# The squares of x's rows ahead of the activations' sums, and the first weight piece on another queue, in a fused encoder layer

## Chip, cores and metric

The kernel runs on one core of one Trainium2 chip. The metric is the device time of one execution in microseconds (us). A core has a matrix engine (TensorE, PE; its weight loads are listed as PEld), VectorE (DVE), ScalarE (ACT), GpSimd (POOL) and SyncE (SP), which only issues transfers here. Each engine runs its own list of instructions in order and waits on semaphores for the others. Transfers (DMAs) are issued by an engine's instruction and carried out by 16 shared DMA engines; the rows named SPq, ACTq and POOLq are the issuing side of those engines.

## What is computed

One layer of a bidirectional encoder on x of shape (512, 1024), float32:

```python
h = _rmsnorm(x, g_pre_mix)
proj = h @ w_in
q, k, v, g, u, sv, a_ret, a_sgu = jnp.split(proj, ...)
y_ret = _retention_branch(q, k, v, g, ret_decay_logit, w_ret_o)
y_sgu = _sgu_branch(u, sv, sgu_ln_g, sgu_ln_b, w_spatial, b_spatial, w_sgu_o)
merged = jax.nn.sigmoid(a_ret) * y_ret + jax.nn.sigmoid(a_sgu) * y_sgu
x = x + _rmsnorm(merged @ w_out, g_post_mix)
h2 = _rmsnorm(x, g_pre_ffn)
x = x + _rmsnorm(_conv_gated_mlp(h2, w_up, conv_w, conv_b, w_down), g_post_ffn)
```

What matters for this change is the first line. The norm divides each row of x by the root of its mean square. The kernel doesn't form h: it multiplies x, scaled by g_pre_mix, with the weights, and applies the factor of each row (`rstd`) to the products afterwards. So the squares of x's rows are needed only when the first products are to be scaled.

## The kernel before

**Numbers in two halves.** All large products are made of three matmuls (`mm3`). Each operand is split into a high half, rounded to the type fp32r by a copy on ScalarE (`copy`, L71), and a low half, the difference, made on VectorE (`tensor_sub` in `split`, L78). Weights come from one array `wall` of 146 blocks of 128 by 1024. `w_block` loads a block (L109), rounds it and forms its low half. Block 0 is loaded in three pieces, of 128, 384 and 512 columns (L122), so that TensorE can start on the first columns early; the first piece is rounded on VectorE (L123), the others on ScalarE. Raw blocks rotate through 4 buffers (one of them is kept by `hold` for the first microseconds), the halves through 9.

**Order of the work.** The text asks for weight blocks ahead of their use (`w_get`). A scheduler in the framework makes one list of instructions for each engine when the program is built: it goes by the place in the text, and takes an instruction from further down when it reckons that those before it aren't ready. Tiles come from pools by tag. The large tag is `blk` (74 tiles of 128 by 512), which serves the halves of x, the scaled copies, the sums, the rows of x, the q and k products and most of the rest; `tmp` has 6 tiles; constants have a tile each. PSUM has 8 banks in rotation (`ps`).

**The stages that the change touches.**
1. The parameters (`part`) are loaded on ScalarE's queue (L173). ScalarE then loads its function table and makes one small copy (`wact`). TensorE runs 18 warm-up matmuls (L213).
2. The q and k projection: for k from 0 to 7, `load_x` brings xT[k] (L189, a block of x transposed) and rounds it with its gain (L191); `x_low` forms the low half (L197); the matmuls of block k go into all 8 PSUM banks, `qk[0]` to `qk[7]` (L227 for block 0, `mm3` at L167 to L169 behind it). In between, `x_scaled` makes a scaled copy `xg[k]` of xT[k] on ScalarE (L204).
3. The activations' sums (`x_forms`, L245 to L260): for each of 4 pairs of scaled copies, four half-width additions on VectorE (L249 to L252), then two splits, whose roundings are on ScalarE and whose low halves are on VectorE. Their results are operands of the gate products (L612), much later.
4. Constants, then the squares by rows (L279 to L285): eight loads of half a row block of x (L282, on SyncE's queue, into `blk` tiles), and for each a Square on ScalarE that adds up along the row (L283). VectorE adds the two halves (L286), and `rsqrt` on POOL (L273, L276) makes `rstd`.
5. The logarithms of the decays (L291 to L312), small work on VectorE.
6. The eight PSUM banks are copied out (`qkraw`, `blk` tiles; L319 on VectorE for odd m, L71 on ScalarE for even m).
7. Four small matmuls (L327) spread rstd over a PSUM bank, which is the first bank that the copies of stage 6 set free. ScalarE copies it to `rbc`, which scales the rotary tables, loaded at L338 and L339.
8. `prep` (rotary) on VectorE, and beside it the first group of `t_group` on TensorE (L430 to L432), which takes four more of those banks.

All later stages (retention, spatial gating, gates, output projection, feed-forward) keep their text.

Of the kernel before, what the change touches and what calls it, by code (L numbers as in the profile page):

```python
# [15 lines left out]
P = 128  # L16
# [24 lines left out]
def tile_block(ctx: ExitStack, tc, xT, x, wall, par, cs, decay, wsp, bsp, gpost, gffn, out):  # L41
    nc = tc.nc
# [5 lines left out]
    def nm(s):  # L48
        uid[0] += 1
        return f"{s}_{uid[0]}"  # L50

    def blk(dt=F32, n="blk", shape=(P, S)):
        return sb.tile(list(shape), dt, tag="blk", bufs=NBLK, name=nm(n))
# [7 lines left out]
    def small(n, w, bufs=2):  # L61
        return sb.tile([P, w], F32, tag=n, bufs=bufs, name=nm(n))
# [4 lines left out]
    def const(n, shape):  # L67
        return sb.tile(list(shape), F32, tag=n, bufs=1, name=n)
# [4 lines left out]
    def as32(t):  # L73
        return t.bitcast(F32)

    def split(hi, lo, src):
        copy(hi, src)
        nc.vector.tensor_sub(lo, src, as32(hi))  # L78
# [6 lines left out]
    i = 0  # L85
# [13 lines left out]
    def raw_tile():  # L99
        return sb.tile([P, 1024], F32, tag="raw", bufs=4, name=nm("raw"))  # L100

    def slot(n, at=0):
        return sb.tile([P, 1088], F32R, tag="w4", bufs=9, name=nm(n))[:, at : at + 1024]

    def w_block(i):
        raw = raw_tile()
        resident = RES0 <= i < RES1 or i >= NW - RES_DOWN
        if i > 0:
            nc.sync.dma_start(raw, wall[i])  # L109
        if resident:  # L110
            hi, lo = [], []
            for c in range(2):
                h_, l_ = blk(F32R, "wh"), blk(F32R, "wl")
                split(h_, l_, raw[:, c * S : (c + 1) * S])
                hi.append(h_)
                lo.append(l_)
        else:
            hi, lo = slot("wh"), slot("wl")
            if i == 0:
                pieces = [slice(0, P), slice(P, S), slice(S, 2 * S)]  # L120
                for f in pieces:
                    nc.sync.dma_start(raw[:, f], wall[i, :, f])  # L122
                    (nc.vector.tensor_copy if f.start == 0 else copy)(hi[:, f], raw[:, f])  # L123
                for f in pieces:
                    nc.vector.tensor_sub(lo[:, f], raw[:, f], as32(hi[:, f]))
            else:
                split(hi, lo, raw)
        return hi, lo
# [24 lines left out]
    def w_get(look=LOOK):  # L153

        i = w_pos[0]
        w_pos[0] += 1
        room = 2 * look + (2 if units[i][0] == "blk" else 0)
        n = sum(w_size(u) for u in units[i : w_pos[1]])
        while w_pos[1] < len(units) and (w_pos[1] <= i or n + w_size(units[w_pos[1]]) <= max(room, 9 if look == LOOK else 0)):
            u = units[w_pos[1]]  # L160
            w_ready[w_pos[1]] = w_block(u[1]) if u[0] == "blk" else w_form(*u)
            w_pos[1] += 1
            n += w_size(u)
        return w_ready.pop(i)
# [6 lines left out]

    part = const("part", [P, NPAR])
    nc.scalar.dma_start(part, par)  # L173


    wact = const("wact", [P, 16])
# [68 lines left out]
    def x_forms(k):  # L245

        a, b = xg[k], xg[k + 4]
        s_ = blk(n="xs")
        nc.vector.tensor_sub(s_[:, T0], a[:, T1], b[:, T1])  # L249
        nc.vector.tensor_sub(s_[:, T1], s_[:, T0], a[:, T0])  # L250
        nc.vector.tensor_sub(a[:, T0], a[:, T0], a[:, T1])
        nc.vector.tensor_add(a[:, T1], b[:, T0], s_[:, T1])  # L252
        for names, s_ in (("S1", "S2"), s_), (("S3", "S4"), a):
            h_, l_ = blk(F32R, "sh"), blk(F32R, "sl")
            split(h_, l_, s_)
            for n, t in zip(names, (T0, T1)):
                forms[n].append((h_[:, t], l_[:, t]))

    for k in range(4):
        x_forms(k)  # L260

    ident = const("ident", [P, P])
    make_identity(nc, ident)
    ones = const("ones", [P, P])
# [5 lines left out]
    def rsqrt(o, v, scale, w):  # L270

        t = small("rs", 16, 4)
        nc.gpsimd.tensor_scalar(  # L273
            out=t[:, :w], in0=v, scalar1=scale, scalar2=EPS, op0=ALU.mult, op1=ALU.add
        )
        nc.gpsimd.tensor_tensor(out=o, in0=t[:, :w], in1=nhalf[:, :w], op=ALU.pow)  # L276
# [9 lines left out]
    nc.vector.tensor_add(ss[:, :NT], ss[:, :NT], ss[:, NT : 2 * NT])  # L286
    rstd = const("rstd", [P, NT])
    rsqrt(rstd, ss[:, :NT], 1.0 / D, NT)


    lgt = const("lgt", [P, 8])  # L291
# [23 lines left out]
    raw = []  # L315
# [582 lines left out]
    for t in range(NT):  # L898
        q = small("q", 2, 4)
        z = sb.tile([P, 1088], F32, tag="w4", bufs=9, name=nm("z"))[:, :D]  # L900
        for n in range(2):
            f = slice(n * S, (n + 1) * S)
# [107 lines left out]
```

## Time and profile before

| | us |
|---|---|
| median of 3 runs | 858.49 (856.82 to 858.81) |
| the profiled execution, its own time | 857.87 |
| its span, first to last instruction | 856.1 |
| PE / DVE / ACT / POOL busy | 838.8 / 547.2 / 377.5 / 70.1 |
| mean granted TensorE clock | 0.993 |

The profile is of one execution. Its rows give the start in us from the span's beginning, the length, the engine, the line of the kernel, the operation, and the tiles written and read, as output<-input. A bracket names how long the engine had been idle and what ended that idle time. An entry like x8 counts instructions put together in one row. The chain of waits goes back from the last instruction, at each step to what released it; what lies on that chain sets the time. The granted clock is 1.00 when TensorE's clock runs at full speed and 0.50 at half.

### The profile page before, as it was taken

Reading aid. Unit: us, or ns where it says so; the run is one execution under the profiler, and the core shown is the slowest. Engines: PE = TensorE matmul, PEld = TensorE weight load, DVE = VectorE, ACT = ScalarE, POOL = GpSimd, SP = SyncE. Lnnn points to the kernel's source line nnn. Section 1 sums busy time; section 2 is a strip of 40 time slices with the busy share of each in tenths; the row PEclk is TensorE's granted clock in tenths of the full one; section 3 lists DMA queues with packets and bytes.
Section 4 is the critical chain, followed back from the end, with each engine's and each line's share of the span. In section 5 each row is a group of like instructions: output and inputs, shape, how many; then the busy total and the mean of one; then the engine's idle time right before and its main releaser. Section 6 shows DMA issues by size and latency. Waiting matters only on the chain.

```text
span 856.1 us, 11249 instructions
## 1 busy us (share of the span) xinstructions
PE 838.8 (98%) x4444; PEld 722.1 (84%) x4444; DVE 547.2 (64%) x846; ACT 377.5 (44%) x605; POOL 70.1 (8%) x75
## 2 busy tenths in 40 slices
PE   8969999999999999999999999999999999999996
PEld 6858888888899999999988898888888888888885
DVE  5767987875698777767764766666666666322304
ACT  6554446444565544344444564444444444211301
POOL 0010000001222011123210100000000000000000
PEclk9989999999999999999999999999999999999999
DMA  8452222120234322222357033222222222222202
GB/s 269 154 200 83 74 75 75 54 95 25 62 99 149 99 99 81 93 99 99 127 162 278 1 96 102 99 98 99 99 99 98 99 97 91 97 90 96 96 1 99
DMA packets 27125, 87.88 MB, mean 103 GB/s; under 512 B 3072, under 2 KB 3712, under 8 KB 27072
## 3 DMA queue, kind: packets, MB, share of 16 engines
q1 hardware_dynamic: 25920, 84.82, 29.5%
q0 software_dynamic: 432, 1.32, 0.6%
q10 hardware_dynamic: 720, 1.02, 0.3%
q8 instruction: 35, 0.57, 0.3%
q14 instruction: 18, 0.15, 0.1%
HBM read 85.05 MB, written 2.10 MB: 102 GB/s over the span
## 4 chain that ended last, share of the span: by engine, by line
PE 94%; DVE 3%; ACT 1%; DMA 1%; issue 0%; POOL 0%; SPq 0%; POOLq 0%; DVEq 0%; ACTq 0%
PE ps L167 15%; PE ps L168 15%; PE ps L169 15%; PE ps L612 11%; PE ps L758 6%; PE ps L759 6%; PE ps L757 6%; PE ps L430 5%; PE ps L431 5%; PE ps L432 5%; DVE wf L78 2%; DMA raw<-wall 1%; PE ps L227 1%; PE ps L682 1%; PE ps L555 0%
## 5 line engine op out<-in xcount | busy, mean ns | idle before, releaser
L78 DVE TENSOR_TENSOR wl<-raw,wh 128x1024 fp32r<-128x1024 f32 (+1 forms) x131 | 149.1, 1149 | 160.4 <-PE ps L168 70.5
L71 ACT ACTIVATE wh<-raw 128x1024 fp32r<-128x1024 f32 (+2 forms) x133 | 129.1, 982 | 100.6 <-PE ps L759 45.3
L169 PE MATMUL ps<-h2h,wl 128*128 128x512 f32 (+1 forms) x384 | 142.3, 371 | 0.0
L168 PE MATMUL ps<-h2l,wh 128*128 128x512 f32 (+1 forms) x384 | 142.2, 371 | 0.0
L167 PE MATMUL ps<-h2h,wh 128*128 128x512 f32 (+1 forms) x384 | 142.2, 372 | 0.0
L71 ACT ACTIVATE wf<-raw 128x512 fp32r<-128x512 f32 x84 | 50.7, 627 | 80.5 <-issue 25.8
L78 DVE TENSOR_TENSOR wf<-raw,wf 128x512 fp32r<-128x512 f32 x84 | 67.3, 818 | 26.8 <-ACT wf L71 26.5
L168 PEld LDWEIGHTS ps<-h2l,wh 128*128 128x128 f32 x384 | 72.3, 188 | 12.6
L167 PEld LDWEIGHTS ps<-h2h,wh 128*128 128x128 f32 x384 | 72.1, 188 | 12.7 <-ACT h2h L823 0.3
L169 PEld LDWEIGHTS ps<-h2h,wl 128*128 128x128 f32 x384 | 72.2, 188 | 12.4
L430 PE MATMUL ps<-wh,xh 128*128 128x512 f32 x192 | 75.3, 392 | 0.0
L431 PE MATMUL ps<-wl,xh 128*128 128x512 f32 x192 | 75.1, 391 | 0.0
L432 PE MATMUL ps<-wh,xl 128*128 128x512 f32 x192 | 74.9, 390 | 0.0
L612 PE MATMUL ps<-sh,wf 128*128 128x256 f32 x384 | 72.8, 280 | 0.2 <-ACT u L71 0.2
L757 PE MATMUL ps<-wh,fh 128*128 128x512 f32 x176 | 68.5, 389 | 0.0
L758 PE MATMUL ps<-wl,fh 128*128 128x512 f32 x176 | 68.5, 389 | 0.0
L759 PE MATMUL ps<-wh,fl 128*128 128x512 f32 x176 | 68.5, 389 | 0.0
L866 ACT ACTIVATE cv<-ps,part 128x512 f32<-128x512 f32 x44 | 34.3, 780 | 76.3 <-PE ps L169 76.3
L612 PEld LDWEIGHTS ps<-sh,wf 128*128 128x128 f32 x384 | 60.8, 188 | 0.9 <-ACT u L71 0.6
L612 PE MATMUL ps<-xh,wf 128*128 128x256 f32 x288 | 54.6, 281 | 0.0
L612 PE MATMUL ps<-sl,wf 128*128 128x256 f32 x192 | 53.6, 279 | 0.0
L612 PEld LDWEIGHTS ps<-xh,wf 128*128 128x128 f32 x288 | 45.5, 188 | 0.4
(240 smaller groups left out, 1532.6 us busy)
## 6 DMA issues: line engine op xcount, KB each, us to landing
raw<-wall SPq DMA_DIRECT2D x145, 512.0 KB, 3.3
x<-x SPq DMA_DIRECT2D x16, 256.0 KB, 6.0
xT<-xT SPq DMA_DIRECT2D x8, 256.0 KB, 5.2
out<-z SPq DMA_DIRECT2D x4, 256.0 KB, 2.0
out<-z ACTq DMA_DIRECT2D x3, 256.0 KB, 2.5
cs<-cs SPq DMA_DIRECT2D x2, 256.0 KB, 3.8
gpm<-gpost POOLq DMA_DIRECT2D x2, 256.0 KB, 3.5
gpf<-gffn POOLq DMA_DIRECT2D x2, 256.0 KB, 3.6
```

Of the source, the lines that this page charges most:

```text
L71: nc.scalar.activation(out=o, in_=i, func=AF.Copy)
L78: nc.vector.tensor_sub(lo, src, as32(hi))
L167: nc.tensor.matmul(o, ah, bh, start=start, stop=False)
L168: nc.tensor.matmul(o, ah, bl, start=False, stop=False)
L169: nc.tensor.matmul(o, al, bh, start=False, stop=stop)
L430: nc.tensor.matmul(acc[t], xh[k][:, c], wh[:, f], start=k == 0, stop=False)
L431: nc.tensor.matmul(acc[t], xh[k][:, c], wl[:, f], start=False, stop=False)
L432: nc.tensor.matmul(acc[t], xl[k][:, c], wh[:, f], start=False, stop=k == KD - 1)
L612: nc.tensor.matmul(o, w_[:, c], a_, start=first and k == n == 0, stop=k == 3 and n == 2, skip_group_check=True,)
L757: nc.tensor.matmul(o, ah, bh, start=k == 0, stop=False)
L758: nc.tensor.matmul(o, ah, bl, start=False, stop=False)
L759: nc.tensor.matmul(o, al, bh, start=False, stop=k == self.nk - 1)
```

## The change

Two edits. The call of `x_forms` for the four pairs moves from ahead of the constants to behind `rsqrt(rstd, ...)`, so that in the text the eight loads and squares of x's rows, their sum and rstd now come ahead of the activations' sums. And the raw buffer of weight block 0 is taken at the very start of the text, where its first piece (128 columns, 64 KB) is issued on ScalarE's queue, behind `part`; the other two pieces stay on SyncE's queue, behind xT[0].

```diff
     def w_block(i):
-        raw = raw_tile()
+        raw = raw_tile() if i else raw0
...
                 for f in pieces:
-                    nc.sync.dma_start(raw[:, f], wall[i, :, f])
+                    if f.start:
+                        nc.sync.dma_start(raw[:, f], wall[i, :, f])
                     (nc.vector.tensor_copy if f.start == 0 else copy)(hi[:, f], raw[:, f])
...
     part = const("part", [P, NPAR])
     nc.scalar.dma_start(part, par)
+    raw0 = raw_tile()
+    nc.scalar.dma_start(raw0[:, 0:P], wall[0, :, 0:P])
...
-    for k in range(4):
-        x_forms(k)
-
     ident = const("ident", [P, P])
...
     rstd = const("rstd", [P, NT])
     rsqrt(rstd, ss[:, :NT], 1.0 / D, NT)
+    for k in range(4):
+        x_forms(k)
```

## The prediction

> **What bounds the kernel now.** I read the page's busy shares first, then the chain of waits around the places the diff touches, then each engine's timeline there, then a table by stretches.
>
> ```profile
> PE 838.8 (98%) x4444; PEld 722.1 (84%) x4444; DVE 547.2 (64%) x846; ACT 377.5 (44%) x605; POOL 70.1 (8%) x75
> ```
>
> TensorE (PE) works through 98% of a span of 856.1 us. So an edit pays only where TensorE stands still or runs at half clock. The chain of waits (start, length, what) shows two such places near the change. The first is the start:
>
> ```profile
> 0.73 0.38 SPq L189
> 1.17 0.42 SPq L122
> 1.64 5.30 DMA raw<-wall
> 6.96 0.53 ACT wh L71
> 7.54 7.17 PE ps L227 x23
> ```
>
> SyncE's queue (SPq) issues xT[0], then the pieces of weight block 0. The second piece (columns 128 to 511) sets the end: 5.30 us in flight, a rounding copy on ScalarE at 6.96, and TensorE starts at 7.54. From there to the end of the projection TensorE is full. In the rows of stretches the columns are length, PE busy, PEld, DVE, ACT, POOL, granted clock, DMA share and GB/s:
>
> ```profile
> 11.46:52.40 40.94, 40.94 (x182) 33.86 (x181) 31.32 (x70) 25.20 (x39) 0.00 (x0) 1.00 0.65 225
> 52.80:59.70 6.90, 0.01 (x1) 0.01 (x1) 3.64 (x6) 6.66 (x17) 1.30 (x3) 0.72 0.55 195
> 59.70:61.50 1.80, 1.80 (x9) 1.80 (x9) 1.24 (x2) 0.00 (x0) 1.76 (x3) 0.50 0.03 9
> ```
>
> The second place is the hole right behind: from 52.80 to 59.70 TensorE does nothing, and then it works at clock 0.50. The chain through that hole:
>
> ```profile
> 52.56 0.24 PE ps L169
> 52.82 1.06 ACT wh L71
> 53.88 3.06 ACT x L283 x10
> 56.94 0.48 ACT qkraw L71
> 57.42 0.62 ACT x L283 x2
> 58.60 1.06 POOL rstd L276
> 59.70 2.08 PE ps L327 x8
> 61.77 0.43 PE ps L430
> ...
> 62.93 0.23 PE ps L430
> ```
>
> ScalarE rounds a weight block (52.82), squares six halves of x's rows (L283, 0.61 us each), copies one sum out of PSUM between them, then POOL makes rstd, and only then may TensorE spread rstd (L327) and begin the next group (L430). (Each square counts twice, with the read of its accumulator: x10 is five.) The squares need x alone, and yet six of eight run after the projection.
>
> Why are the squares so late? SyncE's timeline and the page's list of landings:
>
> ```profile
> 32.12 0.33 SPq L109 DMA_DIRECT2D raw<-wall  x1
> 37.56 0.33 SPq L109 DMA_DIRECT2D raw<-wall  x1
> 43.26 0.33 SPq L109 DMA_DIRECT2D raw<-wall  x1
> 43.64 3.90 SPq L282 DMA_DIRECT2D x<-x  x8
> ```
> ```profile
> x<-x SPq DMA_DIRECT2D x16, 256.0 KB, 6.0
> ```
>
> The eight loads of x's rows are issued from 43.64 to 47.5, behind three weight loads that the text places elsewhere, and take 6.0 us to land. Two squares fit before the weight rounding of 52.82; six stand behind it. The loads need nothing from the chip, so something else held them. My reading: x's rows lie in tiles of the large shared pool (tag blk), and its tiles are handed out in the order of the text, so the loads waited for the sums' tiles. Two rows speak for it:
>
> ```profile
> L657 POOL DMA_DIRECT2D bst<-bsp x1: 626/626/626, 224.5 to 224.5; - x1
> ```
> ```profile
> 62.67 0.33 SPq L655 DMA_DIRECT2D wst<-wsp  x1
> ```
>
> Two neighbouring loads of the text: the one into a blk tile waits until 224.5, although POOL is 8% busy; the one into a tile of its own goes at 62.67.
>
> **The change, part by part.** *1. Squares ahead of the sums.* No instruction is added or removed; eight loads, eight squares, the addition (L286) and POOL's rstd move ahead of the sums (x_forms). By the reading above the loads may now go once the last scaled copy of xT has its tile:
>
> ```profile
> 32.64 1.94 ACT L204 ACTIVATE xg<-xT,part 128x512 f32<-128x512 f32 x3
> ```
> ```profile
> 33.44 0.42 DVE L249 TENSOR_TENSOR xs<-xg,xg 128x256 f32<-128x256 f32 x1
> 36.28 1.23 DVE L78 TENSOR_TENSOR wl<-raw,wh 128x1024 fp32r<-128x1024 f32 x1 [0.44 <-PE ps L168]
> ...
> 49.29 0.69 DVE L78 TENSOR_TENSOR sl<-xg,sh 128x512 fp32r<-128x512 f32 x1
> ...
> 52.65 1.22 DVE L78 TENSOR_TENSOR wl<-raw,wh 128x1024 fp32r<-128x1024 f32 x1 [2.68 <-issue]
> 53.80 1.28 DVE L319 COPY qkraw<-ps 128x512 f32<-128x512 f32 x2
> ```
>
> That tile is given at about 33.9 (the third of three copies from 32.64). On SyncE's queue the loads then stand between the weight loads of 32.12 and 37.56: eight issues at 3.90/8 = 0.49 us fill 33.0 to 37.5. They move past two weight loads (37.56 and 43.26), which delays the first by some tenths; its block is rounded only at 52.82, so that is covered. Landing 6.0 us later, the last square ends near 44, and rstd (0.16 + 0.19 + 1.06 us on DVE and POOL, by the distance from 58.04, where the last square's 0.62 ends, to 59.66) is there near 46. No wait on rstd is left at 52.80.
>
> What is late next? First, the sums. Before, they ran from 33.44 to 49.98 on VectorE, 16.5 us with three weight blocks' low halves among them:
>
> ```profile
> L78 DVE TENSOR_TENSOR wl<-raw,wh 128x1024 fp32r<-128x1024 f32 x3 | 3.7, 1220 | 0.4 <-PE ps L168 0.4
> ```
>
> Without these they take 12.9 us. Now they wait for the tiles of x's rows and start, I estimate, at 36 to 37.5, behind the low half of 36.28. With two low halves (2.4 us) and up to 1 us for ScalarE's eight squares (4.9 us) crossing their splits, they end at 52 to 54. That is the edge of the hole, and the copies of the sums out of PSUM (qkraw, blk tiles too) stand behind them now, where they stood behind the squares before. The old cover for the sums was 10 us of slack up to 59.7; the new one is nearly nothing.
>
> Second, TensorE's next instruction (L327) writes a PSUM bank that the first qkraw copy must empty. That copy is on ScalarE, and the rounding of the weight block, free at 52.82, may stand ahead of it: 1.06 + 0.48 gives 54.36, plus 0.05: TensorE idles from 52.80 to 54.4, 1.6 us. The bound below is 0 (copies made during the projection's last matmuls, since all banks but the last are complete before its end), the bound above is the old hole. I take 1.6, because the sums' estimated end falls on 52 to 54 and the rounding becomes free just there. The next banks follow on VectorE: the low half of 52.65 ends at 53.9, two copies of 0.64 by 55.2, beside L327.
>
> Third, the price of the whole hole. From 52.80 to 62.93 TensorE did L327 (2.08 us at half clock, 1.04 at full, by the clock row) and three matmuls, at full clock 0.23 each as the row at 62.93: together 1.73 us of work in 10.13 us. So 8.4 us are lost there, and 8.4 - 1.6 = **6.8 us** come back, if the clock stays full.
>
> ```profile
> 4.63:8.03 3.40, 1.15 (x6) 0.63 (x4) 1.46 (x3) 0.62 (x2) 0.00 (x0) 1.00 0.86 225
> 8.05:11.44 3.39, 3.39 (x9) 2.38 (x9) 1.53 (x3) 2.36 (x4) 0.00 (x0) 0.50 0.91 350
> ...
> 52.42:55.82 3.40, 0.36 (x2) 0.00 (x0) 2.42 (x3) 3.00 (x8) 0.00 (x0) 1.00 0.59 210
> 55.84:62.64 6.80, 2.94 (x11) 2.75 (x12) 3.69 (x8) 4.44 (x12) 3.06 (x5) 0.50 0.33 118
> ```
>
> These stretches are cut on the grid on which the granted clock changes in this trace; they are multiples of 3.4 us. A stretch with 0.36 us of TensorE work and one with 1.15 of 3.40 were each followed by half clock; full stretches by full clock. With an idle 1.6 us the stretch from 52.42 holds about 1.8 us of work, 0.65 above the nearest row that lost the clock and 1.6 below a full one. I take full clock; losing it costs half of 3.4, 1.7 us. The Trainium skill, "TensorE: Matmul & The Clock Gate", section "What's actually happening", says that the clock falls to half after an idle window of about 3.4 us, in windows that run freely; by that an idle of 1.6 us would lose nothing. The trace is stricter: 2.25 us of idle in a window sufficed at 4.63.
>
> Behind the hole nothing new binds: TensorE's stretch from 62.66 starts with its operands there, and the sums are first read by the products of L612, behind all groups of t_group.
>
> *2. First piece on ScalarE's queue.*
>
> ```profile
> 1.16 1.28 ACT L71 ACT_TABLE_LOAD   x1 [1.16 <-PEq L1000]
> 4.01 0.72 ACT L191 ACTIVATE xh<-xT,part 128x512 fp32r<-128x512 f32 x1 [1.34 <-DMA part<-par]
> 4.18 0.23 DVE L123 CAST wh<-raw 128x128 fp32r<-128x128 f32 x1 [3.17 <-DMA raw<-wall]
> ```
>
> ScalarE spends one issue more (0.42 as L122's) ahead of its table load; 1.34 us of waiting before 4.01 hide it. The piece is issued at about the same time as before, 1.15, so the cast at 4.18 stays. SyncE's queue loses one issue, so the second piece and all behind it go 0.42 us earlier; if its flight stays 5.30, TensorE starts at 7.1 and, being full from there, carries 0.4 to the end. Bounds: +0.42 and, if the extra queue slows the second piece by as much, -0.42, since the trace has no case of both. I take 0.4.
>
> **Sum**: 857.87 (the profiled execution, 1.8 us more than its span) - 6.8 - 0.4 = 850.7. The runs' median is 0.6 higher, by which it would be 851.3. I put 851.0 between.
>
> **Rivals.**
> - *No hole at all.* The sums end by 51 and the copies run before 52.8: the 1.6 us go too, 849.1. For it: all banks but the last are complete before; against it: the sums' estimate.
> - *The clock falls anyway*: 850.7 + 1.7 = 852.4. For it: 1.15 of 3.40 lost it.
> - *The sums become the wait.* If they end at 55 to 57 instead, because ScalarE, where splits stand in line with squares waiting for loads, holds them, the first bank is free 2 to 4 us later than in my sum, and the clock falls: 853 to 856, say 854.5. For it: VectorE's sums and ScalarE's splits alternate, so one late square delays both. Against: ScalarE is busy only 25.20 of 40.94.
> - *Nothing moves.* The build keeps the squares behind the rounding of 52.82 for another reason than mine: only part 2 is left, 857.5.
> - *Slower: the loads stay behind the weight load of 43.26 while the squares stand ahead of the splits.* Then the last x lands at 47.1 + 6.0 = 53.1, its square ends at 53.7, and three quarters of the sums (9.7 us) come after it: 63.4, one copy 64.0, L327 at 64.1 instead of 59.7: 4.4 us lost, less 0.4: 861.9. It decides at a last landing of about 49: 49 + 0.6 + 9.7 + 0.6 is 59.9. Against it: the loads need no tile after 33.9 by my reading.
>
> **How the numbers follow.** Forecast 0.50 (851.0); no hole 0.10; clock 0.08; sums as the wait 0.14; nothing moves 0.09; slower 0.09. A difference under 0.3% (2.6 us) can't be told from no change here. Faster by more: 0.50 + 0.10 + 0.08 + 0.14 = 0.82; within: 0.09; slower: 0.09. The range is 848.5 to 856.0: below, the case without a hole with 0.6 to spare; above, the end of the sums' case. What it leaves out is the last two cases, 0.18.
>
> **What would show it.** In the profile after: L282 issued from about 33 to 38; L283 ended by 45; rstd on POOL before 50, and no wait of L327 on it; what ends L327's wait is a qkraw copy, within 2 us of the projection's end; granted clock 1.00 there; the sums' last split on VectorE at 52 to 54; L227's run of matmuls starting at 7.1. If the loads still go behind 43, my reading of the tiles' order is wrong; if L327 waits over 3 us, the sums are the new wait; if the first matmuls are not earlier, part 2 gives nothing.

## The result and the profile after

The changed kernel takes 856.4 us (median of 12 runs, 854.56 to 860.73), beside 857.73 us (12 runs, 855.76 to 859.86) for the kernel before, run beside it. The ratio is 0.9989 with an interval of 0.9974 to 1.0004: no difference that can be told. Predicted were 851.0 us and faster. The profiled execution took 855.59 us, its span is 853.8 us and its mean granted clock 0.994.

The first half of the mechanism came about. SyncE's timeline and POOL's (start, length, engine, what; a bracket gives the idle time before and what ended it):

```profile
31.46 3.89 SPq L282 DMA_DIRECT2D x<-x  x8
```
```profile
43.38 1.59 POOL L276 TENSOR_TENSOR rstd<-rs,nhalf 128x4 f32<-128x4 f32 x1
```

The eight loads of x's rows are issued from 31.46, where they were issued from 43.64 before, and rstd is ready at 44.97, where it had been ready at 59.66. But TensorE's timeline and the stretches (length, PE, PEld, DVE, ACT and POOL busy, granted clock, DMA share, GB/s) still show the hole:

```profile
49.36 0.39 PE L170 MATMUL ps<-xh,wl 128*128 128x512 f32 x1
55.83 2.05 PE L329 MATMUL ps<-ident,rstd 128*128 128x128 f32 x8 [6.08 <-ACT qkraw L71]
```
```profile
48.40:51.80 3.40, 1.35 (x6) 0.77 (x5) 3.11 (x8) 1.26 (x2) 0.00 (x0) 1.00 0.50 154
51.80:58.60 6.80, 2.77 (x11) 2.61 (x12) 6.04 (x11) 4.81 (x9) 0.00 (x0) 0.50 0.44 157
```

TensorE idles 6.08 us (6.91 before), then again works at half clock. The idle time is ended by ScalarE's first copy out of PSUM, no longer by rstd. The chain of waits through the hole, with the middle left out, says what that copy waited for:

```profile
31.46 3.90 DMA x<-x
35.38 0.03 ACT x L283
...
36.10 0.95 ACT wh L71
37.05 2.99 ACT x L283 x10
...
41.26 0.95 ACT wh L71
42.20 0.61 ACT x L283 x2
42.82 0.53 ACT sh L71
43.37 0.69 DVE sl L78
44.06 0.35 DVE xs L252
...
54.57 0.63 ACT sh L71
55.20 0.49 ACT qkraw L71
55.70 0.14 issue
55.83 2.05 PE ps L329 x8
57.88 0.43 PE ps L432
```

Read from the end: L329 waits for the copy (qkraw), the copy for the last rounding of the activations' sums (sh, 54.57), the sums back to 43.37 for ScalarE's line of squares, and these for the first load of x's rows. The sums have become the wait. VectorE's and ScalarE's timelines show where they lost their time:

```profile
34.44 0.42 DVE L252 TENSOR_TENSOR xs<-xg,xg 128x256 f32<-128x256 f32 x1
...
38.74 1.23 DVE L78 TENSOR_TENSOR wl<-raw,wh 128x1024 fp32r<-128x1024 f32 x1 [2.50 <-PE ps L169]
40.67 0.69 DVE L78 TENSOR_TENSOR sl<-xs,sh 128x512 fp32r<-128x512 f32 x1 [0.71 <-ACT sh L71]
...
43.37 0.69 DVE L78 TENSOR_TENSOR sl<-xg,sh 128x512 fp32r<-128x512 f32 x1 [0.36 <-ACT sh L71]
...
55.23 0.69 DVE L78 TENSOR_TENSOR sl<-xg,sh 128x512 fp32r<-128x512 f32 x1 [0.76 <-ACT sh L71]
```
```profile
35.38 0.63 ACT L283 ACTIVATE x<-x 128x512 f32<-128x512 f32 x1 [3.49 <-DMA x<-x]
...
36.01 1.04 ACT L71 ACTIVATE wh<-raw 128x1024 fp32r<-128x1024 f32 x1
...
40.03 0.61 ACT L71 ACTIVATE sh<-xs 128x512 fp32r<-128x512 f32 x1
```

The additions of the first group begin at 34.44 and are done at 36.24. Their first split needs a rounding on ScalarE, and ScalarE does it only at 40.03: ahead of it in its list stand a square that waits 3.49 us for its load, a weight rounding and five more squares. From 35.38 on ScalarE is never idle until the group's second rounding (42.72 to 43.34) is done: it works off the eight squares, two weight roundings and the group's two roundings. The first group takes from 34.44 to 44.06; a weight block's low half (38.74) runs within it while VectorE waits. The other three, with two weight blocks' low halves between them, take from 43.98 to 55.92.

Where did the time come from? Counting matmuls in both traces, the changed kernel's lead over the kernel before is 3.04 us at the end of the projection, 3.87 us at L329 and 3.98 us behind the first group of t_group. It is 2.97 us at the last matmul, and 2.28 us at the end of the span. So in this pair of executions three quarters of the lead come from the start of the kernel, and the hole itself gave back only 0.9 us.

### The profile page after: what moved, and what is told of

Same layout as the page of the kernel before. It is cut to its first block, busy times and chain, and to the rows that moved or that the text cites. A ratio compares the mean times of both kernels' runs of the same rounds, so it can differ in the third digit from the quotient of the medians.

```text
span 853.8 us, 11250 instructions
## 1 busy us (share of the span) xinstructions
PE 837.8 (98%) x4444; PEld 722.2 (85%) x4444; DVE 547.0 (64%) x846; ACT 377.8 (44%) x605; POOL 70.0 (8%) x75
## 4 chain that ended last, share of the span: by engine, by line
PE 92%; DMA 2%; DVE 2%; ACT 2%; issue 0%; SPq 0%; POOLq 0%; DVEq 0%; ACTq 0%
PE ps L168 14%; PE ps L614 14%; PE ps L169 14%; PE ps L170 14%; PE ps L761 6%; PE ps L760 6%; PE ps L759 6%; PE ps L433 5%; PE ps L432 5%; PE ps L434 5%; DMA raw<-wall 1%; PE ps L684 1%; ACT wh L71 1%; DMA xT<-xT 1%; DVE wl L78 1%; ACT x L283 0%
```

## Experiments

**The theory**, the letter A in the expectations: the copies out of PSUM and the sums take tiles of one tag (`blk`), which are handed out in the order of the text, so the copies can't be made before the sums are done. The sums are late since their splits stand behind the squares in ScalarE's list. The 3 us at the start are chance. **Rivals**: the piece on ScalarE's queue gives those 3 us steadily. The copies are late because ScalarE and VectorE are busy with sums, whatever the tiles. Squares ahead of the sums cost the same with any tiles. And without the hole the time would be lost again further down.

*1. The piece alone* (the sums stay ahead of the constants):

```diff
+    for k in range(4):
+        x_forms(k)
+
     ident = const("ident", [P, P])
...
-    for k in range(4):
-        x_forms(k)
```

> Only the second edit: the first piece on ScalarE's queue, the sums ahead of the squares as before. Theory A (the changed kernel's start gained 3 us in its profile because the second and third piece land earlier, of which 0.4 us is the issue and the rest is chance of transfers and clock): the projection starts at 5.9 to 7.1 and ends at 49.8 to 52.4; the hole behind it keeps its shape, since the squares still wait behind it; the time falls by 0.4 to 3 us, 854.7 to 857.3. Rival B (the queue as such gives the whole 3 us each time): start at 5.9, 3 us less, about 854.7. Rival C (the start's gain is always lost in the hole, since what ends the hole does not hang on the projection's end): no change, 857.7.

Measured: 858.07 us (12 runs), ratio 0.9994, 0.9982 to 1.0007. The hole is that of before, in its place and with its cause (TensorE, window from 49 to 61):

```profile
60.03 1.28 PE L330 MATMUL ps<-ident,rstd 128*128 128x128 f32 x5 [4.34 <-POOL rstd L279]
```

The piece alone gives nothing, so the idea that it steadily gives 3 us falls, and the 0.4 to 3 us of the theory did not come either. Here the projection even ended late, its last matmul at 55.29 instead of 52.40.

*2. The squares alone* (all three pieces on SyncE's queue):

```diff
-        raw = raw_tile() if i else raw0
+        raw = raw_tile()
...
-                    if f.start:
-                        nc.sync.dma_start(raw[:, f], wall[i, :, f])
+                    nc.sync.dma_start(raw[:, f], wall[i, :, f])
...
-    raw0 = raw_tile()
-    nc.scalar.dma_start(raw0[:, 0:P], wall[0, :, 0:P])
```

> Only the first edit: squares ahead of the sums, all pieces on SyncE's queue. Theory A (the wait on rstd is replaced by a wait on the sums: their additions and splits end near 56 whatever the projection does, and the copies of the PSUM banks stand behind them): the projection ends at 52.8, L327 starts near 55.8 to 56.5 instead of 59.7, the hole is 3 to 3.7 us instead of 6.9, and the time falls by 3 to 4 us, to about 854. Then both edits together are hardly better than this one alone, because the earlier end of the projection only makes the hole longer. Rival C (the move itself gives nothing, the 2.3 us in the changed kernel's profile are those of the start): 857.7, within 0.3% of before.

Measured: 856.27 us (12 runs), ratio 0.998, 0.997 to 0.999. This is the whole of what the change gives: 1.7 us. The profile is of the fastest of the 12 runs (854.76).

```profile
55.79 2.04 PE L326 MATMUL ps<-ident,rstd 128*128 128x128 f32 x8 [4.09 <-ACT qkraw L71]
```

The projection's last matmul starts at 51.31 here and at 49.36 in the changed kernel, and yet the hole ends at 55.79 and 55.83. TensorE's earlier end only made the hole longer. The theory had the mechanism and expected a larger gain.

*3. The kernel before, with x's rows in tiles of another tag.* If the tiles' order held the loads, then this one word should free the loads and keep the sums where they were:

```diff
-            xt = blk(n="x0")
+            xt = tmp("x0")
```

> The text order of before (sums ahead of squares, all pieces on SyncE's queue); only x's rows are loaded into the six tiles of tmp instead of blk tiles. Theory A (the blk tiles are handed out in the order of the text, and this alone held the loads, and in the changed kernel the copies out of PSUM): loads issued from about 27 to 36, squares fill ScalarE's gaps and end by 46, the sums end near 50, the copies out of PSUM begin before the projection ends; L327 starts within 1 us of 52.8 and the clock stays full: 7 to 8.4 us less than before, 849.3 to 850.7. Rival D (VectorE and ScalarE have not the time for squares and sums ahead of the projection's end, whatever the order of tiles): the hole stays over 3 us, gain under 4 us, 854 or more.

Measured: 848.53 us (4 runs, 848.07 to 849.46), ratio 0.9891, 0.9874 to 0.9908. In SyncE's, TensorE's and VectorE's timelines:

```profile
27.58 2.10 SPq L282 DMA_DIRECT2D x<-x  x3
```
```profile
52.64 1.05 PE L327 MATMUL ps<-ident,rstd 128*128 128x128 f32 x8
```
```profile
50.58 0.69 DVE L78 TENSOR_TENSOR sl<-xg,sh 128x512 fp32r<-128x512 f32 x1 [0.70 <-ACT sh L71]
```

The first three loads go at 27.58 and the other five at 33.40, instead of 43.64. The sums end at 51.27, and L327 follows the projection without idle time, in 1.05 us instead of 2.08: the clock is full. The lead is 0 at the end of the projection and 8.57 us behind the first group, close to the 8.4 us at which the prediction priced the whole hole.

*4. The changed kernel with x's rows in that other tag.* The squares still stand ahead of the sums; only the tiles differ:

```diff
-            xt = blk(n="x0")
+            xt = tmp("x0")
```

> The changed kernel with one word changed: x's rows in tmp tiles instead of blk tiles. Theory A (not the order of squares and sums in itself, but the blk tiles that they share with the sums makes the sums start and end late): loads from about 24 to 32, squares end before 40, the sums end at 50 to 51, the copies stand right behind them: L327 within 1.5 us of the projection's end, about 848 to 850. Rival E (squares ahead of the splits in ScalarE's queue are enough to push the sums' end to 55 or later): hole over 3 us, 853 to 856.

Measured: 850.27 us (5 runs, 848.16 to 852.87), ratio 0.9911, 0.9895 to 0.9928.

```profile
51.86 1.13 PE L329 MATMUL ps<-ident,rstd 128*128 128x128 f32 x8 [0.88 <-ACT qkraw L71]
```

The loads are no longer late (five are issued from 25.52, three from 31.80), the sums end at 51.95, and the hole shrinks to 0.88 us, in a profile of the fastest of the five runs. VectorE's and ScalarE's rows of the first group:

```profile
30.82 0.42 DVE L252 TENSOR_TENSOR xs<-xg,xg 128x256 f32<-128x256 f32 x1
...
39.50 0.69 DVE L78 TENSOR_TENSOR sl<-xg,sh 128x512 fp32r<-128x512 f32 x1 [0.36 <-ACT sh L71]
```
```profile
35.20 0.62 ACT L71 ACTIVATE sh<-xs 128x512 fp32r<-128x512 f32 x1
...
38.85 0.61 ACT L71 ACTIVATE sh<-xg 128x512 fp32r<-128x512 f32 x1
```

The first group still takes 9.4 us, from 30.82 to 40.19, nearly as in the changed kernel (9.6). The squares stand ahead of its two roundings here too, although the first square waits for no load and later ones at most 0.35 us. In version 3, where the text has the sums first, it takes 5.7 us (33.46 to 39.15). So the squares ahead of the sums cost the splits much the same with these tiles. What the other tag changed is the start: 30.82 instead of 34.44, which is 3.6 of the 4.0 us by which the sums end earlier.

*5. The changed kernel with the copies out of PSUM in tiles of their own.* The sums stay as late as they are; only the copies need no tile behind them (74 `blk` tiles become 66, so that the memory is the same):

```diff
-NBLK = 74
+NBLK = 66
...
-        t = blk(n="qkraw")
+        t = sb.tile([P, S], F32, tag="qk", bufs=8, name=nm("qkraw"))
```

> The changed kernel with the eight copies out of PSUM in tiles of a tag of their own (8 tiles, blk cut from 74 to 66). Squares and sums stay as in the changed kernel. Theory A (the copies wait only because their blk tiles are given after those of the sums): the copies go between the sums as the banks complete, L327 within 0.5 us of the projection's end though the sums still end at 56 or later; the part up to the first v products then gains as e3 does, 6 to 8 us; the whole gains as much unless 66 blk tiles are too few later. Rival F (the copies wait for the engines themselves, which are busy with sums): L327 near 55.8 as in the changed kernel, 856.

Measured: 850.42 us (4 runs, 849.09 to 852.26), ratio 0.991, 0.9894 to 0.9927. TensorE's, ScalarE's and VectorE's timelines:

```profile
54.86 1.05 PE L329 MATMUL ps<-ident,rstd 128*128 128x128 f32 x8
```
```profile
51.36 1.07 ACT L71 ACTIVATE qkraw<-ps 128x512 f32<-128x512 f32 x2
```
```profile
60.48 0.69 DVE L78 TENSOR_TENSOR sl<-xg,sh 128x512 fp32r<-128x512 f32 x1
```

The last low half of the sums ends at 61.17, 5 us later than in the changed kernel, and yet the copies go from 51.36 on and L329 follows the projection's last matmul (54.63) at once. So the copies waited for the order of the tiles alone. That the engines were too busy with sums for the copies falls.

*6. The changed kernel with the sums moved behind the first `prep`*, so that neither loads nor copies wait for them:

```diff
-    for k in range(4):
-        x_forms(k)
...
     prep(0)
+    for k in range(4):
+        x_forms(k)
```

> The changed kernel with the sums moved on, behind the first rotary stage, so that nothing of them stands ahead of the copies out of PSUM. Theory A: squares as in the changed kernel (end near 43), copies out of PSUM done as the banks complete, L327 right behind the projection, clock full: with the start of the changed kernel (projection's end 49.8) 8.4 + 0.4 to 3 us less than before, 846.5 to 849.5. Rival D (the 12.9 us of the sums on VectorE then fall on the rotary stage and the first v products, TensorE waits there for VectorE): a new idle time of TensorE at 75 to 95 of 2 to 8 us eats the gain, 850 to 857.

Measured: 853.74 us (6 runs, 850.13 to 855.43), ratio 0.9942, 0.9919 to 0.9965. The hole is gone: L327 starts at 50.57, directly behind the projection, and the lead is 10.64 us behind the first group. But part of it is given back, as the stretches of TensorE's second group show:

```profile
100.00:110.00 10.00, 9.59 (x50) 7.75 (x48) 7.38 (x18) 6.40 (x13) 1.68 (x2) 1.00 0.30 107
110.00:120.00 10.00, 9.18 (x47) 7.76 (x47) 9.86 (x16) 3.19 (x7) 0.00 (x0) 1.00 0.16 53
```

```profile
106.16 0.50 PE L430 MATMUL ps<-wh,xh 128*128 128x512 f32 x1 [0.41 <-DVE kt L413]
...
110.90 0.50 PE L430 MATMUL ps<-wh,xh 128*128 128x512 f32 x1 [0.82 <-DVE vl L441]
```

In both stretches TensorE now waits for VectorE. The lead falls to 7.79 us by 220 us. The sums don't vanish: from 67 to 87 us they stand in VectorE's way there. The rival of a loss further down holds in part. This profile is of the fastest of the six runs (850.13); the others reach 855.43 and have no profile, so it isn't shown why the median lies 3.6 us above it.

*7 and 8. Version 3 with the piece on ScalarE's queue*, that is the kernel before with edit 2 (its lines in `w_block` as in the change) and the other tag; run twice, the second time beside version 3 itself:

```diff
+    raw0 = raw_tile()
+    nc.scalar.dma_start(raw0[:, 0:P], wall[0, :, 0:P])
...
-            xt = blk(n="x0")
+            xt = tmp("x0")
```

> e3 (text order of before, x's rows in tmp) with the first piece on ScalarE's queue as well. Here no hole stands behind the projection that could swallow the start, so the difference to e3 is the worth of the second edit alone. Theory A (0.4 us of issue, the rest chance of transfers and clock): 0 to 1 us under e3's 848.53, 847.5 to 848.5. Rival B (the queue gives 3 us each time): about 845.5.

> e5 once more, beside e9. Theory A: 847.5 to 850, the same as e9 within 0.2%, with a wider spread of its runs. Rival B: 1 us or more under e9.

Measured: 849.18 us (6 runs, 846.95 to 853.56), ratio 0.99, 0.9878 to 0.9922; then 851.55 us (6 runs, 846.83 to 853.35), ratio 0.9904, 0.988 to 0.9928. ScalarE's timeline at the start, with the rounding of the second piece (384 columns) and of the third (512), in the second of these:

```profile
4.69 0.51 ACT L71 ACTIVATE wh<-raw 128x384 fp32r<-128x384 f32 x1
8.68 0.63 ACT L71 ACTIVATE wh<-raw 128x512 fp32r<-128x512 f32 x1 [3.48 <-DMA raw<-wall]
```

*9. Version 3 once more*, same kernel:

> e3 once more, beside e10 on one chip, to weigh the second edit where no hole can swallow it. Theory A (the piece on ScalarE's queue lets the second piece land up to 1 us earlier, but the third piece and the granted clock decide when block 0 is done, and they vary from run to run): 848 to 849.5, the same as e10 within 0.2%. Rival B (the queue gives a steady gain): e10 is 1 us or more faster.

Measured: 848.77 us (6 runs, 848.06 to 851.13), ratio 0.9885, 0.9867 to 0.9903.

```profile
6.59 0.52 ACT L71 ACTIVATE wh<-raw 128x384 fp32r<-128x384 f32 x1 [1.91 <-DMA raw<-wall]
8.24 0.63 ACT L71 ACTIVATE wh<-raw 128x512 fp32r<-128x512 f32 x1 [1.13 <-DMA raw<-wall]
```

The same rounding in the profiled run of the changed kernel:

```profile
5.31 0.52 ACT L71 ACTIVATE wh<-raw 128x384 fp32r<-128x384 f32 x1 [0.57 <-DMA raw<-wall]
6.04 0.64 ACT L71 ACTIVATE wh<-raw 128x512 fp32r<-128x512 f32 x1 [0.21 <-DMA raw<-wall]
```

The piece on ScalarE's queue does bring the second piece earlier. But the third, for which TensorE then waits in seven of the eight profiles with this piece (0.56 to 3.58 us), is rounded anywhere between 6.0 and 9.4 us. In the medians version 3 with the piece is slower than without it: 849.18 beside 848.53 us, then 851.55 beside 848.77, which had been expected within 0.2% of each other. But the runs of each pair overlap.

*10 and 11. The changed kernel and the kernel before, profiled a second time*, to see what of the first profiles was chance:

> The changed kernel once more, for a second look at its start and its hole. Theory A: the projection's end differs by up to 3 us from the first look (49.8), the end of the hole (55.8) by less, since it hangs on the sums; the time is then 855 to 858. If projection's end and hole's end move together, the sums are not what ends the hole.

> The kernel before once more, for a second look at its start and its hole. By what was seen so far: block 0 is finished at 13.5 to 14.6, the projection ends at 51.7 to 52.9, and L327 starts 6.5 to 7 us behind its end, since the squares wait for the weight block that the projection's end sets free.

Measured: 858.91 and 858.03 us (one execution each). TensorE's rows at the hole, the changed kernel first:

```profile
58.03 2.04 PE L329 MATMUL ps<-ident,rstd 128*128 128x128 f32 x8 [4.71 <-ACT qkraw L71]
```
```profile
60.12 1.22 PE L327 MATMUL ps<-ident,rstd 128*128 128x128 f32 x4 [6.91 <-POOL rstd L276]
```

The causes are the same as in the first profiles. But the changed kernel's projection now has its last matmul at 52.93 instead of 49.36, and the hole's end has moved 2.2 us with it. The expectation named that as a sign against the sums as the wait. But the sums moved too: their additions begin at 38.01 instead of 34.44 and their last low half at 57.43 instead of 55.23, and the copy that ends the hole still stands behind their last rounding. What was wrong is that the sums would end near 56 whatever the projection does. The changed kernel's last matmul of all is 0.38 us later than that of the kernel before. The start of 49.36 was a lucky one. Over the eight profiles with the piece on ScalarE's queue the third piece is rounded at 6.04, 6.92, 6.96, 7.14, 8.29, 8.68, 8.94 and 9.43 us, and over the five with all pieces on SyncE's queue at 7.67, 7.83, 8.23, 8.24 and 8.25. The projection's last matmul starts at 49.36 to 55.29 us, mean 52.26, in the eight, and at 51.31 to 52.83, mean 52.27, in the five. The clock divides the eight: where the third piece is rounded by 7.14 us, TensorE keeps its clock at the start and the last matmul starts by 50.61; where it is rounded from 8.29 us on, one or two stretches of 3.4 us at half clock follow, and it starts from 52.93 on. Edit 2 is worth nothing on average in these profiles, and widens the spread.

## Why the prediction was wrong, step by step

- *The tiles' order holds the loads, and they go early once it doesn't.* Right: issued from 31.46 (forecast 33), last square at 42.73 (near 44), rstd at 44.97 (46). Experiment 3 shows the order of the tiles as the cause, with one word changed.
- *The sums end at 52 to 54.* **This is the step that failed**: "With two low halves (2.4 us) and up to 1 us for ScalarE's eight squares (4.9 us) crossing their splits, they end at 52 to 54." They began even earlier than assumed, at 34.44. From there 12.9 of their own and 2.4 for two low halves would end at 49.8; they ended at 55.92. So the crossing cost 6.2 us and not up to 1. The whole of it is in the first group: 9.6 us from 34.44 to 44.06, where a quarter of 12.9 is 3.2. (The two low halves counted are those of 46.30 and 51.99; the one of 38.74 runs while the split waits.) The prediction counted the squares' work, 4.9 us, and thought that it would slip in between. In fact ScalarE's list has six squares and a weight rounding ahead of the first split's rounding, which could have begun at 35.31 and begins at 40.03, and the other two squares and another weight rounding ahead of the second one's. The wait for the first load, 3.49 us in the row of 35.38, brings this block to where the sums want ScalarE, but it isn't needed for the cost: in experiment 4 nearly nothing is waited for and the first group takes 9.4 us all the same. What the order in the list costs shows beside experiment 3, where the squares stand between the splits: 5.7 us.
- *What ends L327's wait is a copy.* Right by name, wrong in size: 6.08 us instead of 1.6, since the copies stand behind the sums. Experiment 5 shows that only the tiles' order held them.
- *The clock stays full.* Wrong, as follows from the longer hole: a stretch with 1.35 of 3.40 us of work was followed by half clock. Where the hole is gone (experiments 3 and 5) the four matmuls take 1.05 us.
- *The hole's price of 8.4 us.* Right: its removal gave 8.57 us in experiment 3. It was just not removed: 0.9 us came back in the first profile (lead of 3.04 at the projection's end, 3.98 behind the first group), 1.2 in the second (-0.54 to 0.62), 1.8 in experiment 2 (1.08 to 2.91).
- *Edit 2 gives 0.4.* Wrong in its reason. The forecast had TensorE full from its first matmul on. In fact it then waits for the third piece in seven of the eight profiles with this edit (3.03 us in that of the row of 8.68, where ScalarE waits 3.48), and the mean gain is 0.
- *The rival in which the sums become the wait*, with a chance of 0.14, is what happened, end of the sums at 55 to 57 and the lost clock included. It gave 853 to 856, say 854.5, and its upper end left 856.4 just outside the range. It took its gain from L329's start alone. Where that was 3.87 us earlier, 3.04 were the start's chance; where the start was ordinary, in the second profile, L329 began only 1.67 us earlier.
- *The slower rival* did not come: the loads went ahead of the weight load that it put them behind.

The median of the changed kernel fits its parts: 1.7 us from edit 1 (experiment 2), nothing from edit 2 (experiment 1), against 1.3 us measured.

**Left open**: between 235 and 275 us the changed kernel loses 1.0 us of its lead, in both of its profiles, and no other kernel does so. In TensorE's stretch from 240 to 256 us it does fewer matmuls than the kernel before, at full clock and without idle time, before first and then after:

```profile
240.00:256.00 16.00, 16.00 (x144) 1.00 0.28 94
```
```profile
240.00:256.00 16.00, 16.00 (x138) 1.00 0.30 99
```

No experiment was aimed at it. In its two profiles a matmul starts on average 0.118 us after the one before it in this stretch, in the other eleven 0.113. The kernel before takes up the quicker pace at a short pause of TensorE (0.28 us between two starts, at 235.09); the changed kernel has the same pause (at 231.11) and does not. The cause isn't known.

The best version is number 3, the order of before with x's rows in another tag: 848.5 and 848.8 us in two batches, 1.1% faster than before, with neither edit of the change.

## What to carry to other kernels

When a stage is moved ahead, look up what then stands behind it on each engine's list, and count the whole block of work there as a delay, until a trace shows that it slips in between: here eight squares of 4.9 us, with two weight roundings among them, delayed the splits behind them by 6.2. When tiles of one tag serve unrelated stages, the order of the text becomes an order of execution; here moving the text only passed the wait on to the next user of the tag, the copies, while another tag for the rows (experiment 3) or for the copies (experiment 5) took the hole away. And a lead that shows in one profiled execution is to be looked for in a second one before it is credited to an edit.

- **What loses the clock.** Cut on the grid of its changes, each trace shows which stretches of 3.4 us were followed by half clock. Two of those nearest to the bound are the start of version 3, where half clock followed, and that of experiment 4, where it didn't:

```profile
5.42:8.83 3.41, 1.57 (x6) 0.97 (x6) 1.03 (x3) 1.15 (x2) 0.00 (x0) 1.00 0.83 320
8.83:12.24 3.41, 3.41 (x9) 2.64 (x8) 2.42 (x4) 2.95 (x4) 0.00 (x0) 0.50 1.01 353
```
```profile
4.95:8.36 3.41, 1.99 (x8) 1.29 (x8) 2.34 (x5) 1.15 (x2) 0.00 (x0) 1.00 0.81 239
8.36:11.77 3.41, 3.41 (x17) 2.78 (x16) 0.89 (x1) 1.76 (x3) 0.00 (x0) 1.00 1.01 387
```

With 1.57 of 3.41 us of work the clock fell, with 1.99 it stayed: the second column, and the granted clock of the next row. The 1.8 us on which the prediction put full clock lie between the two, where nothing here decides. The Trainium skill, "TensorE: Matmul & The Clock Gate", section "What's actually happening", lets the clock fall after an idle window of about 3.4 us; these rows agree on the window's length, but the clock falls here behind windows that were nearly half full of work.
- **The order of landings.** With the first piece on ScalarE's queue the second one is rounded earlier in all eight profiles (4.64 to 5.31 us, against 5.80 to 6.96 in the five), and the third anywhere from 6.04 to 9.43. The Trainium skill, "DMA: Bandwidth & Descriptors", section "Issuing engines are not separate DMA queues", expects only the issuing time to be saved by several issuing engines; that was 0.42 us here, by the row of L122's issue. In the means the second piece was rounded 1.6 us earlier, 4.91 against 6.51, so issuing time alone does not account for it; what does is not shown.
